# Lower weight halves of q, k, v and the gates by an adding DMA, in place of a GpSimd subtraction

## The chip, the cores and the metric

The kernel runs on one core of a Trainium2 chip. The metric is the device time of one execution in microseconds (us). TensorE (PE) multiplies, VectorE (DVE) and ScalarE (ACT) work element by element, GpSimd (POOL) does so as well, and SyncE (SP) only issues DMAs here. Every engine works through its own instructions in order; what it needs from another engine or from a DMA it waits for on a semaphore, and everything behind the waiting instruction waits with it.

## What is computed

One layer of a hybrid encoder on 512 tokens of width 1024, float32. A projection `w_in` (1024 x 4096) of the modulated, normalised input gives q, k, v, the input u of a state-space branch and two sets of gates. The part that the change touches is this:

```python
h = _normalize(x) * (1.0 + sc_m) + sh_m
proj = h @ w_in
q, k, v, u, g_sb, g_ssm = jnp.split(proj, IN_SPLITS, axis=-1)
y_sb = stick_breaking_attention(q, k, v) @ w_sb_up
y_ssm = s5_branch(u, ...) @ w_ssm_up
merged = jax.nn.sigmoid(g_sb) * y_sb + jax.nn.sigmoid(g_ssm) * y_ssm
y = merged @ w_out
```

After it come a residual with layer norm, a SwiGLU channel mixer of hidden width 2816, and a second residual with layer norm.

## The kernel before

**Splitting.** TensorE multiplies in a rounded float32 form (F32R). To keep accuracy each operand is taken as a sum of an upper part (the value rounded to F32R) and a lower part (the value less the upper part), and `mm3` (L151 on) makes three matmuls of each product: upper by upper, upper by lower, lower by upper; all stand on L149 in the trace.

**Units of weights.** `unit` (L170) brings in 512 KB of weights as a tile of 128 x 1024 float32, `raw`, by a DMA of SP (L146), has ACT round it into `whi` (L177, a cast) and an engine given by the caller write `wlo = raw - whi` (L159, `sub`). There are 8 `raw` buffers (shared with the modulation weights `ra` and with tiles `ce` of the state-space branch) and 4 each of `whi` and `wlo`. A `raw` buffer is free for the next load when the last reader is done with it. All loads stand on SP in the program's order.

**Stages.** Until about 94 us: layer norm, modulation, the columns of u, and the first q and k tiles, beside the sines and cosines of the state-space branch, whose arguments DVE prepares (L395 to L472) and ACT evaluates (L424, L425). From 94 to about 180 us: four state-space slices (`ssm_slice`, L561: complex products on DVE and POOL at L555 to L558, two scans on DVE at L642 and L643), and between them q, k and v. From there to about 340 us: four pairs of attention heads; after each head two gate tiles (`gate_tile`); from 266 us pieces of later modulation vectors on DVE (`ada_acc`, L244). Then merge, GLU, up and out projections, and from 470 us the channel mixer.

**Who gets what.** `qk_tile` (6 units), `v_tiles` (2 x 2 units) and `gate_tile` (16 units) hand `G`, which is GpSimd, to `unit`: 26 units in all. I number the gate tiles 0 to 15. GLU, up, out and the channel mixer hand in engines by tables (`ENG`, `FENG`), mostly DVE. A scheduler places each instruction by priorities (streams "ssm", "qkv", "feed", "attn", "gates" and others) and by its own cost estimates, so the order on an engine can move when an instruction is replaced.

Of the kernel before, what the change touches and what calls it, by code (L numbers as in the profile page):

```python
# [16 lines left out]
AF = mybir.ActivationFunctionType  # L17
ALU = mybir.AluOpType

P = 128  # L20
# [61 lines left out]
def _build(tc, I, out):  # L82
    nc = tc.nc
    V, G = nc.vector, nc.gpsimd
    tt, ts, stt = V.tensor_tensor, V.tensor_scalar, V.scalar_tensor_tensor
    act, acopy = nc.scalar.activation, nc.scalar.copy
    cnt = [0]

    def nm(s):
        cnt[0] += 1  # L90
        return f"{s}_{cnt[0]}"
# [4 lines left out]
    @contextmanager  # L96
    def prio(name):

        old = tc.cur_priority
        tc.cur_priority = streams[name]  # L100
        yield
        streams[name] = tc.cur_priority
        tc.cur_priority = old
# [28 lines left out]
    def get(dt=F32):  # L132

        i = places.popleft()
        ap = const.tile([P, 512], dt, tag=f"s{i}", name=nm(f"s{i}"))
        tiles[id(ap)] = (i, ap)
        return ap

    def put(*aps):
        for ap in aps:  # L140
            places.append(tiles.pop(id(ap))[0])
# [3 lines left out]
    def load(o, i):  # L145
        return tc.keep_in_program_order(nc.sync.dma_start(out=o, in_=i))  # L146
# [4 lines left out]
    def mm3(o, a, b, start, stop):  # L151

        r = mm(o, a[0], b[0], start, False)
        mm(o, a[0], b[1], False, False)
        mm(o, a[1], b[0], False, stop)
        return r

    def sub(dst, a, b, eng=V):
        return eng.tensor_tensor(dst, a, b, ALU.subtract)  # L159

    def split(x, n=512, eng=V, keep=False):

        h, l = get(F32R), get(F32R)
        acopy(h[:, :n], x[:, :n])  # L164
        sub(l[:, :n], x[:, :n], h[:, :n], eng)
        if not keep:
            put(x)
        return h, l

    def unit(view, a, b, eng=V):  # L170

        with prio("feed"):
            raw = wp.tile([P, D], F32, tag="raw", name=nm("raw"), bufs=NRAW)
            load(raw.rearrange("p (a b) -> p a b", a=a), view)
            hi = wp.tile([P, D], F32R, tag="whi", name=nm("whi"), bufs=NHI)
            lo = wp.tile([P, D], F32R, tag="wlo", name=nm("wlo"), bufs=NHI)
            acopy(hi, raw)  # L177
            sub(lo, raw, hi, eng)
        return hi.rearrange("p (a b) -> p a b", a=a), lo.rearrange("p (a b) -> p a b", a=a)

    def slot_unit(view, a, b, eng=V):
# [11 lines left out]
    w_in, w_glu, w_up, w_sb = rows128(I["w_in"]), rows128(I["w_glu"]), rows128(I["w_ssm_up"]), rows128(I["w_sb_up"])  # L193
# [103 lines left out]
    with prio("first"):  # L297
# [11 lines left out]
        hT = hpairs  # L309
# [205 lines left out]
    def fbank():  # L515
        fcnt[0] += 1
        return banks[6 + fcnt[0] % 2]

    def fm_one(view, h, K=KC, o=None, eng=V):

        w = unit(view, K, P, eng) if K == KC else view
        o = fbank() if o is None else o
        for kc in range(K):
            mm3(o, [x[:, kc, :] for x in w], h[kc], kc == 0, kc == K - 1)
        return o
# [6 lines left out]
    def evac_q(p_, i, dst, scale):  # L532
        with prio("feed"):
            act(dst[i], p_, AF.Copy, scale=scale)
# [131 lines left out]


    def qk_tile(i):
        o = fm_one(w_in[:, :, 256 + P * i:256 + P + P * i], hT, eng=G)
        if i < 2:  # L670
            evac_q(o, 2 + i, qT, 0.125)
        else:
            evac_q(o, i - 2, kT, 1.0)

    def v_tiles(i):
        us = [unit(w_in[:, k:k + 4, 1024 + 256 * i:1280 + 256 * i], 4, 256, G) for k in (0, 4)]
        for m2 in range(2):
            o = fbank()
            for m in range(2):
                tk = slice((2 * m2 + m) * P, (2 * m2 + m + 1) * P)  # L680
                for kc in range(KC):
                    mm3(o[:, m * 256:(m + 1) * 256], [a[:, tk] for a in hT[kc]],
                        [x[:, kc % 4, :] for x in us[kc // 4]], kc == 0 and m == 0, kc == KC - 1)
            with prio("feed"):
                for h in range(2):
                    acopy(vT[2 * i + h].rearrange("p (k c) -> p k c", k=NT)[:, 2 * m2:2 * m2 + 2, :],
                          o.rearrange("p (m c) -> p m c", m=2)[:, :, h * P:(h + 1) * P])

    def gate_w(i):
        col = (3072, 2048)[i // 8] + P * (i % 8)  # L690
        return w_in[:, :, col:col + P]
# [4 lines left out]
    def gate_tile(i, eng):  # L696
        lst = (gs, gb)[i // 8]
        o = fm_one(gate_w(i), hT, eng=eng)
        with prio("feed"):
            g = gpre.pop(0) if gpre else get()  # L700
            acopy(g, o)
        lst.append(g)

    with prio("ssm"):
        ys = []
    dense = [lambda i=i: qk_tile(i) for i in range(6)] + [lambda i=i: v_tiles(i) for i in range(2)]
    for s in range(4):
        with prio("ssm"):
# [69 lines left out]
    def later(at):  # L778

        with prio("later"):  # L780
            for _ in range(LATER.get(at, 0)):
                i = len(pieces)
                pieces.append(at)
                if i % 2 == 0:
                    (gm_acc if i < 4 else sf_acc).append(get())
                if i < 4:
                    ada_gate(2, i, gm_acc[i // 2][:, i % 2 * 256:i % 2 * 256 + 256])
                    continue
                j = i - 4
                ada_acc(sf_acc[j // 2][:, j % 2 * 256:j % 2 * 256 + 256], w_ada[:, :, 3 * D + j * 256:3 * D + j * 256 + 256], 256)  # L790
# [3 lines left out]
    for hp in range(4):  # L794
        with prio("attn"):
            at = get()

            q_, k_, kl = ([get(F32R), get(F32R)] for _ in range(3))
            for a in range(2):
                r, r2 = HEAD[a], HEAD[1 - a]  # L800
                acopy(q_[a][r, :], qT[hp][r, :])
                sub(q_[a][r2, :], qT[hp][r, :], q_[a][r, :])
                acopy(k_[a][r, :], kT[hp][r, :])
                acopy(k_[a][r2, :], kT[hp][r, :])
                sub(kl[a][r, :], kT[hp][r, :], k_[a][r, :])
                sub(kl[a][r2, :], kT[hp][r, :], k_[a][r, :])
            put(qT[hp], kT[hp])
            vs = [get(F32R), get(F32R)]
            for a in range(2):
                v4 = vs[a].rearrange("p (k a d) -> p k a d", k=NT, a=2)  # L810
                src = vT[hp].rearrange("p (k c) -> p k c", k=NT)[:, :, 64 * a:64 * a + 64]
                acopy(v4[:, :, 0, :], src)
                sub(v4[:, :, 1, :], src, v4[:, :, 0, :])
            put(vT[hp])
        for a in range(2):
            with prio("attn"):
                for i, (q0, layout) in enumerate(HALVES):
                    half_head(a, q_, k_, kl, vs, at, q0, layout, banks[3 * a + i:3 * a + 1 + 2 * i])
            for g in range(2):
                i = 4 * hp + 2 * a + g  # L820
                with prio("gates"):
                    gate_tile(i, G)
                later(("gate", i))
        put(*q_, *k_, *kl, *vs)
        with prio("attn"):
            attnT.append(split(at))
# [24 lines left out]
    with prio("mix"):  # L851
# [4 lines left out]
        for m in range(4):  # L856
            if m % 2 == 0:
                w = unit(glu_w[m // 2], 4, 256)
            o = bk.get()
            fm_one([x[:, :, m % 2 * P:(m % 2 + 1) * P] for x in w], yS, 4, o)  # L860
            g = get()
            sigmoid(g, o, bias=bglu[:, m:m + 1])
            bk.put(o)
            tt(g, g, yT[m], ALU.mult)
            yG.append(split(g))
            later(("glu", m))
# [4 lines left out]
        for i in range(4):  # L871
            w = unit(up_w[i][0], 4, 256)
            for m in range(2):
                g = gs[2 * i + m]
                sigmoid(g, g)
                o = bk.get()
# [4 lines left out]
            for m in range(2):  # L881
                g, g2 = gb[2 * i + m], gs[2 * i + m]
                sigmoid(g, g)
                o = bk.get()
# [403 lines left out]
```

## Time and profile before

| quantity | value |
|---|---|
| time, median of 3 runs | 841.86 us (839.55 to 842.65) |
| the profiled execution: its time | 841.87 us |
| its span in the trace | 840.2 us |
| PE busy | 760.7 us (91%) |
| DVE busy | 637.8 us (76%) |
| ACT busy | 416.7 us (50%) |
| POOL busy | 190.9 us (23%) |
| mean granted TensorE clock | 0.966 |

The profiled execution lies 0.01 us from the median, so lengths of its trace can be set against the median as they are; 1.7 us of its time lie outside the span. The page also gives the span in 40 slices, the chain of work that ended last, the costliest groups of instructions and the DMAs. Further views of the trace give the busy time by stage, one engine's instructions in order of time with what ended its idle time, and one tile's instructions.

### The profile page before, as it was taken

To read this page: it belongs to the slowest core of one execution; us is meant where nothing else is said; L and a number is where in the kernel's file an instruction comes from. 1 tells how busy PE (TensorE), PEld (TensorE's weight loads), DVE (VectorE), ACT (ScalarE), POOL (GpSimd) and SP (SyncE) were. 2 spreads that over 40 slices of the span, in tenths; PEclk is the share of its full clock that TensorE was granted. 3 is DMA by queue.
4 is the path that set the end of the run, shared out by engine and by line. 5 is a ranking of instruction groups with operands and counts; after the bars stand their busy time and mean duration, and the time that the engine had idled before them with its cause. 6 is when DMAs were issued, how large, how long until landed. Compare 5 with 4: busy or idle time off the path is not lost.

```text
span 840.2 us, 12264 instructions
## 1 busy us (share of the span) xinstructions
PE 760.7 (91%) x4767; PEld 667.5 (79%) x4767; DVE 637.8 (76%) x975; ACT 416.7 (50%) x689; POOL 190.9 (23%) x161
## 2 busy tenths in 40 slices
PE   3969896899999888699998589999999999999995
PEld 2858686897888577588886589999999999888884
DVE  5599778789677998688879988767778777533267
ACT  4234623454887665883526294444445556632211
POOL 1451626662532443100464000000000000000013
PEclk9989999899999999899999699999999999999998
DMA  9960004420002471770972003414445334441001
GB/s 275 354 176 26 1 1 136 116 76 26 1 1 83 147 228 53 240 251 28 348 238 87 0 2 102 150 52 151 151 152 181 116 107 150 148 154 48 1 26 75
DMA packets 95754, 97.86 MB, mean 116 GB/s; under 512 B 4040, under 2 KB 85968, under 8 KB 95696
## 3 DMA queue, kind: packets, MB, share of 16 engines
q1 hardware_dynamic: 95552, 96.82, 36.6%
q8 instruction: 37, 0.61, 0.3%
q10 hardware_dynamic: 144, 0.26, 0.1%
q14 instruction: 21, 0.17, 0.1%
HBM read 94.97 MB, written 2.10 MB: 116 GB/s over the span
## 4 chain that ended last, share of the span: by engine, by line
PE 61%; DVE 24%; issue 4%; ACT 4%; DMA 4%; SPq 2%; POOL 1%; POOLq 0%; DVEq 0%; ACTq 0%
PE b L149 60%; DVE s L244 3%; DVE s L159 2%; SPq L146 2%; DVE s L469 1%; DMA s<-w_in 1%; DMA ra<-w_ada 1%; DVE s L621 1%; DVE wlo L159 1%; DVE raw L1042 1%; ACT s L424 1%; DVE s L642 1%; DVE s L402 1%; DVE st L280 1%; ACT s L425 1%
## 5 line engine op out<-in xcount | busy, mean ns | idle before, releaser
L149 PE MATMUL b<-h,whi 128*128 128x256 f32 (+1 forms) x896 | 217.4, 332 | 18.8 <-DVE h L159 9.4
L159 DVE TENSOR_TENSOR wlo<-raw,whi 128x1024 fp32r<-128x1024 f32 x103 | 129.5, 1264 | 69.1 <-ACT whi L177 37.1
L149 PEld LDWEIGHTS b<-h,whi 128*128 128x128 f32 x896 | 151.2, 191 | 33.4 <-DVE h L159 9.6
L149 PE MATMUL b<-s,whi 128*128 128x256 f32 (+1 forms) x800 | 166.7, 307 | 6.7 <-ACT whi L177 6.7
L149 PE MATMUL b<-h,wlo 128*128 128x256 f32 (+1 forms) x448 | 147.9, 331 | 0.0
L149 PEld LDWEIGHTS b<-s,whi 128*128 128x128 f32 x800 | 129.5, 190 | 16.6 <-ACT whi L177 7.0
L149 PE MATMUL b<-whi,s 128*128 128x512 f32 (+1 forms) x392 | 122.5, 390 | 0.0
L149 PE MATMUL b<-s,wlo 128*128 128x256 f32 (+1 forms) x400 | 121.2, 305 | 0.8 <-DVE wlo L159 0.8
L159 DVE TENSOR_TENSOR s<-s,s 128x512 fp32r<-128x512 f32 (+4 forms) x112 | 89.2, 802 | 37.0 <-PE b L149 18.1
L1049 ACT CAST whi<-raw 128x1024 fp32r<-128x1024 f32 x70 | 72.7, 1050 | 75.5 <-PE b L149 43.3
L177 ACT CAST whi<-raw 128x1024 fp32r<-128x1024 f32 x66 | 68.9, 1048 | 80.9 <-PE b L149 66.2
L159 POOL TENSOR_TENSOR wlo<-raw,whi 128x1024 fp32r<-128x1024 f32 x33 | 84.5, 2572 | 63.5 <-ACT whi L177 62.7
L149 PEld LDWEIGHTS b<-h,wlo 128*128 128x128 f32 x448 | 85.6, 191 | 7.2 <-POOL wlo L159 0.4
L1228 POOL TENSOR_TENSOR s<-s,s 128x512 f32<-128x512 f32 x6 | 8.6, 1431 | 356.6 <-DVE s L1227 356.6
L149 PE MATMUL b<-s,s 128*128 128x128 f32 (+2 forms) x438 | 81.9, 317 | 6.1 <-DVE s L159 3.8
L149 PEld LDWEIGHTS b<-whi,s 128*128 128x128 f32 x392 | 73.3, 188 | 16.6
L164 ACT CAST s<-s 128x512 fp32r<-128x512 f32 (+1 forms) x106 | 57.8, 570 | 49.4 <-DVE s L744 13.7
L149 PEld LDWEIGHTS b<-s,s 128*128 128x128 f32 x438 | 68.8, 192 | 15.9 <-DVE s L159 4.4
L149 PEld LDWEIGHTS b<-s,wlo 128*128 128x128 f32 x400 | 75.3, 188 | 4.5 <-DVE wlo L159 1.0
L149 PE MATMUL b<-wlo,s 128*128 128x512 f32 (+1 forms) x196 | 76.5, 390 | 0.0
L244 DVE SCALAR_TENSOR_TENSOR s<-ra,ca,s 128x256 f32<-128x256 f32 x88 | 58.3, 681 | 2.8 <-DMA ra<-w_ada 2.2
L159 POOL TENSOR_TENSOR s<-s,s 128x512 fp32r<-128x512 f32 (+1 forms) x32 | 39.5, 1246 | 78.9 <-ACT s L164 56.1
(244 smaller groups left out, 1111.8 us busy)
## 6 DMA issues: line engine op xcount, KB each, us to landing
raw<-w_ffn_in SPq DMA_DIRECT2D x44, 512.0 KB, 4.3
ra<-w_ada SPq DMA_DIRECT2D x32, 512.0 KB, 6.0
raw<-w_in SPq DMA_DIRECT2D x26, 512.0 KB, 4.7
raw<-w_ffn_out SPq DMA_DIRECT2D x22, 512.0 KB, 3.4
wa<-w_ada SPq DMA_DIRECT2D x12, 512.0 KB, 7.7
raw<-w_out SPq DMA_DIRECT2D x12, 512.0 KB, 6.3
s<-x SPq DMA_DIRECT2D x16, 256.0 KB, 4.2
wa<-w_ada SPq DMA_DIRECT2D x8, 256.0 KB, 4.9
```

What stands on the lines that cost most here:

```text
L146: return tc.keep_in_program_order(nc.sync.dma_start(out=o, in_=i))
L149: return nc.tensor.matmul(o, lhsT, rhs, start=start, stop=stop, skip_group_check=True, **kw)
L159: return eng.tensor_tensor(dst, a, b, ALU.subtract)
L164: acopy(h[:, :n], x[:, :n])
L177: acopy(hi, raw)
L244: stt(dst, r_, ca[:, k:k + 1], init if k == 0 else dst, ALU.mult, ALU.add)
L280: V.bn_stats(st[:, i, :], x)
L402: e.scalar_tensor_tensor(p_, n, -c, p_, ALU.mult, ALU.add)
L424: act(o, a, AF.Abs, bias=b)
L425: sins.append(act(o, o, AF.Sin, scale=-1.0, bias=hpi_c))
L1049: acopy(hi, x)
L1228: G.tensor_tensor(z[h], z[h], l2b[h], ALU.add)
```

## The change

For the 26 units of q, k, v and the gates the callers hand in `None`. `unit` then lets ACT write the negated rounded value into `wlo` (an ACTIVATE with scale -1), and GpSimd issues a DMA that reads `raw` and adds it onto `wlo`. The sum is `raw - whi`, as before. GpSimd's 26 subtractions go; 26 ACT instructions and 26 DMAs on GpSimd's queue come. Five lines of code come in, one of them blank, so every line below shows a number higher by 5 after the change.

```diff
             acopy(hi, raw)
-            sub(lo, raw, hi, eng)
+            if eng is None:
+                act(lo, raw, AF.Copy, scale=-1.0)
+                G.dma_start(out=lo, in_=raw, accum_op=ALU.add)
+            else:
+                sub(lo, raw, hi, eng)
...
-        o = fm_one(w_in[:, :, 256 + P * i:256 + P + P * i], hT, eng=G)
+        o = fm_one(w_in[:, :, 256 + P * i:256 + P + P * i], hT, eng=None)
...
-        us = [unit(w_in[:, k:k + 4, 1024 + 256 * i:1280 + 256 * i], 4, 256, G) for k in (0, 4)]
+        us = [unit(w_in[:, k:k + 4, 1024 + 256 * i:1280 + 256 * i], 4, 256, None) for k in (0, 4)]
...
-                    gate_tile(i, G)
+                    gate_tile(i, None)
```

The order on SP stays as it is. On the others three places matter.

GpSimd, where the third pair of q and k tiles and the second slice's `ce` tiles (its output matrices) are prepared. Before, the two subtractions stand ahead of four memsets:

```order
L159 TENSOR_TENSOR wlo_1365<-raw_1362,whi_1364 128x1024 [waits PE_49,DMAHW5_49,Activation_49,Pool_49]
L159 TENSOR_TENSOR wlo_1396<-raw_1393,whi_1395 128x1024 [waits DMAHW6_49,PE_49,Activation_49]
L614 MEMSET s_155_943 128x512 [waits DVE_49]
L595 MEMSET ce_1458 128x640 [waits Pool_49]
L595 MEMSET ce_1460 128x640 [waits Pool_49]
L569 MEMSET s_170_1062 128x512 [waits PE_49,Activation_49]
```

Now, with the DMAs in their place:

```order
L619 MEMSET s_155_943 128x512 [waits DVE_49,PE_49,Pool_49]
L181 DMA wlo_1369<-raw_1366 128x1024 [waits DMAHW5_49,PE_49,Activation_49]
L600 MEMSET ce_1464 128x640 [waits DMASW4_49,DMASW2_49]
L181 DMA wlo_1401<-raw_1398 128x1024 [waits DMAHW6_49,PE_49,Activation_49]
L600 MEMSET ce_1466 128x640 [waits DMASW5_49,DMASW3_49]
L574 MEMSET s_170_1064 128x512 [waits PE_49]
```

The memset of s_155 moved ahead; each `ce` memset, whose buffer was a `raw` one, now waits for adding DMAs to land (DMASW), one of which was issued by the row just ahead of it.

TensorE, at the first v unit (whi_1545, wlo_1546; after the change whi_1551, wlo_1552). Before:

```order
L149 MATMUL b_70<-ce_1098,s_186_1113 128x128
L149 MATMUL b_73<-whi_1545,h_64 128x256 [waits Activation_49]
L149 MATMUL b_72<-whi_1545,h_64 128x256 [waits Activation_49]
L149 MATMUL b_73<-wlo_1546,h_64 128x256 [waits Pool_49]
L149 MATMUL b_73<-whi_1545,h_65 128x256
```

Now:

```order
L149 MATMUL b_70<-ce_1100,s_186_1115 128x128
L149 MATMUL b_73<-whi_1551,h_64 128x256 [waits Activation_49]
L149 MATMUL b_72<-whi_1551,h_64 128x256
L590 MATMUL b_70<-ident,s_136_861 128x128 [waits Activation_49]
L590 MATMUL b_70<-ident,s_136_861 128x128 x3
L149 MATMUL b_73<-wlo_1552,h_64 128x256 [waits DMASW6_49]
```

The first matmul on the lower part waits for the adding DMA, and four small transposes have moved ahead of it.

ACT, at the end of the sines and cosines and the evacuation of the first q tile (L534 brings finished q tiles out of PSUM: s_114 and s_115, whose columns were multiplied with u's, then s_116, the first `qk_tile`). Before, the row of L534 that empties b_71 is followed by the small copies of L543 and then by the next cast:

```order
L534 ACTIVATE s_115_840<-b_71 128x512 [waits PE_49]
L543 COPY s_135_860<-b_69 128x4x32 [waits DVE_49]
L543 COPY s_137_862<-b_66 128x4x32 [waits DVE_49]
L543 COPY s_137_862<-b_67 128x4x32 [waits DVE_49]
L543 COPY s_137_862<-b_68 128x4x32 [waits DVE_49]
L543 COPY s_137_862<-b_69 128x4x32 [waits DVE_49]
L177 CAST whi_1364<-raw_1362 128x1024 [waits DMAHW5_49,PE_49,Pool_49]
```

Now:

```order
L539 ACTIVATE s_115_840<-b_71 128x512 [waits PE_49]
L548 COPY s_137_862<-b_66 128x4x32 [waits DVE_49]
L548 COPY s_137_862<-b_67 128x4x32 [waits DVE_49]
L610 COPY s_153_931<-s_138_881 128x512 [waits DVE_49,Pool_49]
L178 CAST whi_1368<-raw_1366 128x1024 [waits DMAHW5_49,PE_49]
L539 ACTIVATE s_116_841<-b_73 128x512 [waits PE_49]
```

A copy that belongs to the first slice, s_153, now stands ahead of the cast and of the evacuation that frees b_73.

## Rows read from the trace of the kernel before

**Rows 1.** Busy us by stage (PE, PEld, DVE, ACT, POOL), granted clock, DMA share, GB/s:

```profile
42.00:96.00 54.00, 42.81 (x226) 34.94 (x224) 49.48 (x132) 27.34 (x48) 20.87 (x19) 0.91 0.28 79
96.00:134.00 38.00, 36.41 (x206) 31.34 (x206) 28.49 (x47) 15.23 (x28) 18.50 (x19) 0.96 0.09 28
134.00:206.00 72.00, 62.25 (x424) 57.59 (x424) 62.64 (x82) 30.61 (x56) 39.62 (x30) 0.93 0.32 89
206.00:268.00 62.00, 61.52 (x348) 53.80 (x349) 43.02 (x64) 50.33 (x98) 25.17 (x18) 1.00 0.01 2
268.00:340.00 72.00, 61.91 (x302) 50.40 (x301) 65.57 (x103) 46.68 (x89) 28.42 (x19) 0.95 0.51 153
```

**Rows 2.** GpSimd's subtractions until 345 us: durations in ns (min/median/max), starts, and who waited:

```profile
L159 POOL TENSOR_TENSOR wlo<-raw,whi x26: 2342/2409/3207, 49.2 to 317.4; 128x1024 fp32r<-128x1024 f32 x26
...
who waited for it (us, times):
...
  PEld b L149: 2.1, 2
  PE b L149: 1.5, 1
```

**Rows 3.** DVE in order of time, 49 to 58 us: start, us, instruction, count:

```profile
49.28 7.82 DVE L469 TENSOR_SCALAR s<-s,s 128x128 f32<-128x128 f32 x5
...
57.96 0.27 DVE L469 TENSOR_SCALAR s<-s,s 128x128 f32<-128x128 f32 x1
```

**Rows 4.** DVE groups by form, 48 to 345 us: busy us, mean ns, idle before:

```profile
L244 DVE SCALAR_TENSOR_TENSOR s<-ra,ca,s 128x256 f32<-128x256 f32 x53 | 40.1, 775 | 2.6 <-DMA ra<-w_ada 2.2
...
L469 DVE TENSOR_SCALAR s<-s,s 128x128 f32<-128x128 f32 x16 | 13.1, 902 | 0.0
```

**Rows 5.** The chain that ended last, 42 to 100 us: start, us, what:

```profile
74.52 1.34 ACT s L424 x2
...
87.49 0.31 DVE s L483
...
95.71 0.51 ACT s L534
96.26 4.10 PE b L149 x11
```

**Rows 6.** DVE in order of time from 95.5 us, at the first slice's products:

```profile
95.89 5.13 DVE L555 TENSOR_TENSOR s<-s,s 128x256 f32<-128x256 f32 x2
```

**Rows 7.** PE in order of time, 134 to 148 us, with idle time and its releaser:

```profile
134.16 0.39 PE L149 MATMUL b<-wlo,h 128*128 128x256 f32 x1 [1.50 <-POOL wlo L159]
...
147.59 1.11 PE L578 MATMUL b<-ident,s 128*128 128x128 f32 x4 [4.37 <-DVE s L558]
```

**Rows 8.** Busy us in the stretch with the longest of these waits, columns as in rows 1:

```profile
145.00:152.00 7.00, 4.41 (x21) 4.41 (x22) 6.85 (x13) 1.72 (x4) 1.60 (x2) 0.51 0.27 75
```

**Rows 9.** PE in order of time, 276 to 302 us:

```profile
276.50 0.74 PE L149 MATMUL b<-h,whi 128*128 128x512 f32 x2 [1.83 <-ACT whi L177]
...
278.95 0.79 PE L149 MATMUL b<-h,wlo 128*128 128x512 f32 x1
...
301.45 0.56 PE L149 MATMUL b<-s,s 128*128 128x256 f32 x3 [3.40 <-DVE s L159]
```

**Rows 10.** DVE in order of time, 279 to 285 us:

```profile
279.57 4.95 DVE L244 SCALAR_TENSOR_TENSOR s<-ra,ca,s 128x256 f32<-128x256 f32 x3
...
284.92 0.47 DVE L244 SCALAR_TENSOR_TENSOR s<-ra,ca,s 128x256 f32<-128x256 f32 x1
```

**Rows 11.** The page's group of `whi` casts: busy us, mean ns, idle before:

```profile
L177 ACT CAST whi<-raw 128x1024 fp32r<-128x1024 f32 x66 | 68.9, 1048 | 80.9 <-PE b L149 66.2
```

**Rows 12.** DMA issues by tile: count, KB each, median us from issue to landing:

```profile
raw<-w_in SPq DMA_DIRECT2D x26, 512.0 KB, 4.7
raw<-w_ffn_out SPq DMA_DIRECT2D x22, 512.0 KB, 3.4
...
raw<-w_ssm_up SPq DMA_DIRECT2D x4, 512.0 KB, 8.2
```

## The prediction

> **What bounds the kernel now.** I read the busy time by stage first [rows 1]. TensorE fills 61.52 of 62 us between 206 and 268 us and 36.41 of 38 between 96 and 134: there nothing else matters. It idles 11.2 us from 42 to 96, 9.75 from 134 to 206 and 10.1 from 268 to 340, and in each of these the granted clock is below 1 too. What it idles for is seen in its instructions in order of time: mostly DVE, 4.37 us in one place, 3.40 in another [rows 7, 9]. Why DVE is late is seen in DVE's own rows: an L469 that takes 0.27 us takes 1.56 on average in a row of five [rows 3], an L244 takes 1.65 beside 0.47 [rows 10]. Each such stretch lies on top of a subtraction of GpSimd, of which there are 26 of 2.41 us from 49 to 317 us [rows 2]. GpSimd is hardly disturbed (its longest is 3.21), DVE all but stops. So the change removes 26 x 2.41 = 62.7 us in which DVE could not use two inputs, and brings a transfer that GpSimd issues, whose length no row shows.
>
> **The new chain of a unit.** Cast, negated copy, DMA. The copy has the cast's size, so 1.05 us [rows 11]. For the landing D of an adding DMA of 512 KB I take bounds from the plain loads of that size [rows 12]: at the low end 3.4 us, the shortest median; at the high end 16.4, twice the 8.2 of the slowest, since the adding DMA must bring in two pieces of 512 KB. I take 6.8, twice 3.4: that load has rows of 4 KB, as `raw` to `wlo` has, while the slower ones have short rows. GpSimd's subtraction took 2.4, so a unit whose lower part is used at once is late by 1.05 + D - 2.4 = D - 1.35: 5.45 us, from 2.05 to 15.05.
>
> The Trainium skill bears on D: in "DMA: Bandwidth & Descriptors", section "Anatomy of one DMA", a GpSimd-issued DMA is fitted by 2.0 us plus the bytes over 436 GB/s. For 512 KB this would be an estimate of 3.2 us, and the sum below would then end near 827. The fit is of transfers that don't add, and no row here shows one that does.
>
> **Where the later arrival shows.** For most units nowhere: of 26 lower parts TensorE's matmuls waited for one and its weight loads for two [rows 2]; counted unit by unit, those of q and k lie ready 16 us or more before use, and those of the gates until 268 us 14 or more. Two places have no slack. At the first v unit TensorE waits 1.50 us for the subtraction [rows 7]; its load waits for a buffer, so nothing brings it forward. At gate tile 10, the first after 268 us, TensorE waits 1.83 us for the cast, and the lower part is used at 278.95 [rows 9], within 0.1 us of its being ready. Gate tiles 11 to 15 have 3 to 7 us, which 5.45 about uses up. So two units pay: 2 x (D - 1.35) = 10.9 us.
>
> **What comes back, stage by stage.**
>
> 42 to 96 us. DVE's 16 L469 take 13.1 us [rows 4] where 16 x 0.27 = 4.3 would do: 8.8 gone. So the first sine can start on ACT at about 65.7 instead of 74.52 [rows 5]. What is late next: the last piece of h, which ACT gets from TensorE, and 4 negated copies (4.2 us) on ACT. I let the sines end at 79 instead of 87.49, and the first slice's products follow, ready near 89.7 since two L555 no longer take 5.13 us [rows 6]. But ACT now has the copy s_153, which waits for these products, ahead of the cast and of the evacuation that frees b_73: 89.7 + 0.5 + 1.0 + 0.5 = 91.7 (copy and evacuation as L534's 0.51, the cast) against 96.26, when TensorE begins the next tile [rows 5, 11]. Gain 4.6, between 2 (the copy late) and 8 (the whole stall).
>
> 96 to 134. TensorE is full; the gain is carried. The first v unit: -5.45, balance -0.8. GpSimd's two `ce` memsets wait for landings that it has itself just asked for, 2D = 13.6 us instead of 4.9 of subtractions; the second slice needs them some 30 us later, so this costs nothing unless D nears 15.
>
> 134 to 206. Idle 9.75 us and 0.07 of 72, 5.0, of lost clock [rows 1]: after the 4.37 us wait the granted clock is 0.51, the lower of its two levels (1.2 of 2.4 GHz), for 7 us [rows 7, 8]. The idle is DVE's chain of slices, which loses its stops. A wait of 5 us at the v unit will bring the low clock once more: 7 us at half speed cost 3.4. So 9.75 + 5.0 - 3.4 = 11.4 at most; I take 10. Balance +9.2.
>
> 206 to 268. DVE's stops are hidden here, TensorE being full. ACT has 50.33 of 62 and gets four negated copies, 4.2 us, between exponentials that TensorE's order rests on: -1. Balance +8.2. Gate tile 10: -5.45, balance +2.8.
>
> 268 to 340. DVE is busy 65.57 of 72 us. The 53 L244 take 40.1 us where 0.47 each makes 24.9 [rows 4, 10]: 15.2 of stops, of which part stays, as GpSimd keeps the subtractions of the attention weights. I count 11.7 at the units. TensorE's idle for DVE, such as 3.40 us [rows 9], and the lost clock (0.05 x 72 = 3.6) are about 11; I let half come back, 5. Balance +7.8. Loads of the later pieces, which come through 8 shared buffers, are the next to be late.
>
> After 340 only 7 subtractions of GpSimd are left, untouched, and all is shifted as it is. Sum: 4.6 + 10 - 1 + 5 - 10.9 = +7.7, and 841.9 - 7.7 is about 834 us. The ends of D give 14.5 faster (827) and 11.5 slower (853). These lengths are of an execution of 841.87 us, 0.01 from the median, so the sum is taken from the median as it is.
>
> **The rivals.**
>
> All of DVE's stops come back. If D is near 3.4 (14.5) and the two stages with 9.75 + 5.0 and 10.1 + 3.6 us of idle and clock return most of it, 3 to 10 us more: 815 to 825, say 820. For it: the chain of waits runs through DVE almost without a break in both. Against it: buffers and loads are close behind.
>
> The landing is late. From 18.6 = 2 (D - 1.35), that is D = 10.7, the two waits eat what the four stages give. At D = 13 they cost 23.3, gate tiles 11 to 15, with their 3 to 7 us, each wait some more, and the low clock follows each wait: 847 to 855, say 850, slower. For it: SP's loads run beside, a load with 8.2 us is in the rows, and the units are read twice. Against it: the share of time in which the 16 DMA engines are busy is only 0.27 to 0.32 there [rows 1, 8].
>
> GpSimd's issuing is held up by DVE. In this kernel: if the issue must find a gap in DVE's work, which is busy 62.64 of 72 and 65.57 of 72 us with instructions of 0.27 to 1.65 us back to back [rows 1, 3, 10], each DMA is late by several of them, 2 to 5 us: D = 9 to 12, 838 to 845 by the sum, say 842. Its only row here speaks against it: GpSimd's subtractions, run into by DVE all the time, took 3.21 at most beside 2.41 [rows 2]. The Trainium skill, "SBUF — State Buffer", section "Who interferes with whom", has this as a rule: a DMA "stalled" by a DVE op was one issued by GpSimd, whose writing of descriptors is starved. No row of before shows such a DMA.
>
> The change doesn't do what it says. If issuing occupies GpSimd as the subtraction did, DVE's stops remain by half: 18.6 / 2 - 10.9 = 1.6 slower, 843.5.
>
> **How the numbers follow.** A change of 0.5%, 4.2 us, is about what a measurement of this kernel can tell from none. The forecast, 828 to 838, has 0.40. All stops return, 0.16, also faster. No difference by a half-done removal or by DVE holding up the issue, 0.12 and 0.08. Slower, by a late landing 0.19 and by DVE holding it up further 0.05. So faster 0.56, same 0.20, slower 0.24. The range reaches from 818, in the middle of the first rival, to 850, the middle of the late landing; about 0.08 and 0.10 are outside.
>
> **What would show it.** In the changed kernel's profile L469, L555, L637 and L244 must fall to their short durations; an L244 of 1.6 us on a landing refutes the main step. ACT's group of negated copies must be 26 of about 1.05 us. At the first v unit and at gate tile 10 TensorE's wait for the DMA must be about 5 us longer than the wait before; each gives D, cast's end to wait's end less 1.05. TensorE should start the second q tile at about 92 us, and the stage that ran from 134 to 206 be shorter by about 10. The prediction is wrong if D is over 10, if the DMAs of GpSimd queue behind each other, or if DVE's stops were only where TensorE did not wait.

## The result, and the profile after

The changed kernel takes 831.05 us (median of 4 runs, 828.48 to 832.43) where the kernel before takes 841.17 us beside it; the ratio is 0.9877, with a 95% interval of 0.9843 to 0.991. Run once more beside later experiments it gave 0.9895 (0.9877 to 0.9913). It is about 1.1% faster. The forecast was 834, the range 818 to 850. The profiled execution is the shortest of its four, 828.48 us with a span of 826.8, so its trace shows some 2.5 us more gain than the median does.

The busy times by stage (columns as in rows 1) stand against [rows 1]:

```profile
42.00:96.00 54.00, 46.50 (x244) 38.20 (x245) 44.17 (x143) 34.95 (x59) 18.01 (x20) 0.94 0.53 123
96.00:134.00 38.00, 33.48 (x197) 28.80 (x196) 25.83 (x48) 15.04 (x27) 13.56 (x18) 0.95 0.30 69
134.00:206.00 72.00, 72.00 (x499) 67.00 (x499) 45.78 (x85) 50.48 (x85) 25.49 (x31) 0.98 0.70 156
206.00:268.00 62.00, 57.75 (x304) 48.75 (x303) 39.48 (x71) 50.75 (x99) 16.70 (x18) 0.94 0.33 83
268.00:340.00 72.00, 60.66 (x286) 48.97 (x287) 44.32 (x87) 49.92 (x86) 17.23 (x18) 0.89 0.72 197
```

From 134 to 206 us TensorE no longer idles at all (72.00 of 72, before 62.25), and DVE is busy 45.78 us where it was 62.64, though it makes more instructions. From 268 to 340 DVE falls from 65.57 to 44.32, but TensorE's busy time does not rise and its granted clock falls to 0.89.

DVE's groups by form from 48 to 345 us answer [rows 4]; the lines are 5 higher:

```profile
L249 DVE SCALAR_TENSOR_TENSOR s<-ra,ca,s 128x256 f32<-128x256 f32 x54 | 26.8, 520 | 2.6 <-DMA ra<-w_ada 1.9
...
L474 DVE TENSOR_SCALAR s<-s,s 128x128 f32<-128x128 f32 x16 | 3.7, 287 | 0.0
L560 DVE TENSOR_TENSOR s<-s,s 128x256 f32<-128x256 f32 x8 | 3.7, 474 | 10.7 <-ACT s L610 8.7 <-PE b L149 2.0
L642 DVE TENSOR_TENSOR s<-s,s 128x512 f32<-128x512 f32 x4 | 2.8, 688 | 0.0
```

The last two lines are the other two that the prediction named, L555 and L637; before, in the same view:

```profile
L555 DVE TENSOR_TENSOR s<-s,s 128x256 f32<-128x256 f32 x8 | 8.4, 1066 | 5.0 <-ACT s L605 4.9
L637 DVE TENSOR_TENSOR s<-s,s 128x512 f32<-128x512 f32 x4 | 4.9, 1232 | 0.0
```

The 16 small products take 3.7 us in place of 13.1, the modulation pieces 26.8 for 54 in place of 40.1 for 53. The stops by the 26 units are gone. The prediction had named an L244 of 1.6 us on a landing as what would refute it, and there is one piece of this length, at 271.65 us, while an adding DMA is under way (270.01 to 274.54). But it lies on two of GpSimd's subtractions of the attention weights, which the change leaves as they were (DVE, then GpSimd):

```profile
271.65 1.79 DVE L249 SCALAR_TENSOR_TENSOR s<-ra,ca,s 128x256 f32<-128x256 f32 x1
```

```profile
270.58 2.58 POOL L159 TENSOR_TENSOR s<-s,s 128x512 fp32r<-128x512 f32 x2
```

The pieces at 269.70 and 270.23 us, on the same landing, take 0.49 us each, so it doesn't refute. What came in their place is seen by the tile `wlo`, until 345 us (the counts, durations in ns, who waited for whom, and the time from issue to landing):

```profile
L180 ACT ACTIVATE wlo<-raw x26: 1050/1057/1087, 48.9 to 309.5; 128x1024 fp32r<-128x1024 f32 x26
L181 POOL DMA_DIRECT2D wlo<-raw x26: 833/866/2042, 50.2 to 310.9; - x26
...
  POOL ce L600: 9.3, 3
  PEld b L149: 5.1, 3
  PE b L149: 4.0, 3
...
DMA to landing us min/median/max: 4.5/5.0/8.1
```

The copy costs the 1.05 us that was assumed. The landing, which no row of before showed, is 5.0 us in the median, between the low end of 3.4 and the 6.8 that I took. TensorE waits for a lower part three times. The first is at the first v unit (start, us, instruction, idle before it); it answers [rows 7]:

```profile
127.07 0.48 PE L149 MATMUL b<-whi,h 128*128 128x256 f32 x2
131.33 1.12 PE L590 MATMUL b<-ident,s 128*128 128x128 f32 x4 [3.78 <-ACT s L623]
132.73 0.58 PE L149 MATMUL b<-wlo,h 128*128 128x256 f32 x1 [0.28 <-DMA wlo<-raw]
```

The long part of the wait is not put down to the DMA but to ACT's copies at L623, which the transposes ahead of the lower part need. ACT's rows say why they are late:

```profile
125.79 1.04 ACT L178 CAST whi<-raw 128x1024 fp32r<-128x1024 f32 x1 [1.25 <-DMA raw<-w_in]
126.74 1.05 ACT L180 ACTIVATE wlo<-raw 128x1024 fp32r<-128x1024 f32 x1
127.70 1.03 ACT L178 CAST whi<-raw 128x1024 fp32r<-128x1024 f32 x1
128.64 1.05 ACT L180 ACTIVATE wlo<-raw 128x1024 fp32r<-128x1024 f32 x1
129.60 1.41 ACT L623 COPY s<-b 32x512 f32<-32x512 f32 x3
```

Two negated copies stand ahead of them, 2.1 us. Had they been early, TensorE would have waited for the landing instead, which came 1.4 us after them. The stretch that follows runs mostly at the lower level of the clock (1.2 of 2.4 GHz), 0.54 in the mean, which over 7.5 us loses 3.5 (columns as in rows 1; first the changed kernel, then e9, an experiment below in which that wait is gone):

```profile
130.00:137.50 7.50, 5.88 (x27) 5.48 (x28) 7.36 (x15) 1.24 (x4) 0.84 (x1) 0.54 0.94 203
```

```profile
130.00:137.50 7.50, 7.50 (x67) 7.50 (x66) 7.34 (x17) 3.08 (x6) 0.00 (x0) 1.00 0.50 143
```

The other two waits for a lower part are at gate tiles 10 and 12; the first answers the row at 278.95 of [rows 9]:

```profile
269.49 0.80 PE L149 MATMUL b<-h,wlo 128*128 128x512 f32 x1 [0.29 <-DMA wlo<-raw]
...
297.77 0.80 PE L149 MATMUL b<-h,wlo 128*128 128x512 f32 x1 [3.40 <-DMA wlo<-raw]
```

To see where time was won, I set the starts of the same matmuls side by side (us; e5, e9, e10 and e8 are experiments below). A scheduler may move other work past such a mark, so single steps of one or two microseconds say little; in the trace of e11, the changed kernel run again, the lower part of gate tile 10 is used at 271.45 us, 2.0 later than here.

| mark on TensorE | before | after | e5 | e9 | e10 | e8 |
|---|---|---|---|---|---|---|
| third q/k tile, first matmul | 96.26 | 91.59 | 91.54 | 91.91 | 91.57 | 91.91 |
| first v unit, first with the lower part | 134.16 | 132.73 | 128.46 | 129.07 | 129.00 | 128.16 |
| gate tile 0, first matmul | 181.00 | 169.39 | 160.98 | 160.25 | 160.21 | 160.86 |
| gate tile 3, first matmul | 209.67 | 194.79 | 185.97 | 185.98 | 185.94 | 185.96 |
| gate tile 9, first matmul | 261.07 | 246.17 | 237.75 | 237.02 | 236.98 | 234.68 |
| gate tile 10, first with the lower part | 278.95 | 269.49 | 261.10 | 267.38 | 264.47 | 267.96 |
| gate tile 15, end | 338.55 | 329.22 | 311.13 | 326.13 | 313.59 | 312.71 |
| first GLU matmul | 349.26 | 335.56 | 322.56 | 335.05 | 331.91 | 334.46 |

### The profile page after: what moved, and what is told of

Its sections match the earlier page's. It is cut to its first block, busy times and chain, and to the rows that moved or that the text cites. A ratio compares the mean times of both kernels' runs of the same rounds, so it can differ in the third digit from the quotient of the medians.

```text
span 826.8 us, 12325 instructions
## 1 busy us (share of the span) xinstructions
PE 761.7 (92%) x4767; PEld 667.0 (81%) x4767; DVE 585.1 (71%) x975; ACT 438.5 (53%) x715; POOL 147.2 (18%) x161
## 3 DMA queue, kind: packets, MB, share of 16 engines
q1 hardware_dynamic: 95552, 96.82, 37.2%
## 4 chain that ended last, share of the span: by engine, by line
PE 51%; DVE 4%; ACT 2%; issue 2%; DMA 1%; POOL 0%; SPq 0%; POOLq 0%; DVEq 0%; ACTq 0%
PE b L149 51%; DVE st L285 1%; DMA raw<-w_glu 1%; ACT s L974 0%; DVE s L972 0%; ACT whi L1054 0%; DVE mv L290 0%; DVE h L159 0%; DVE s L946 0%; ACT s L844 0%; DVE s L1232 0%; POOL s L159 0%; DVE s L955 0%; DVE s L943 0%; ACT s L1074 0%
## 5 line engine op out<-in xcount | busy, mean ns | idle before, releaser
L149 PE MATMUL b<-h,whi 128*128 128x256 f32 (+1 forms) x896 | 217.9, 333 | 13.1 <-DVE h L159 8.2
L159 DVE TENSOR_TENSOR wlo<-raw,whi 128x1024 fp32r<-128x1024 f32 x103 | 127.5, 1243 | 72.2 <-ACT whi L178 38.9
L149 PEld LDWEIGHTS b<-s,whi 128*128 128x128 f32 x800 | 128.6, 189 | 16.5 <-ACT whi L178 5.7
L159 DVE TENSOR_TENSOR s<-s,s 128x512 fp32r<-128x512 f32 (+4 forms) x112 | 79.0, 716 | 59.4 <-PE b L149 22.1
L149 PEld LDWEIGHTS b<-whi,s 128*128 128x128 f32 x392 | 73.2, 188 | 16.5
L1047 DVE TENSOR_TENSOR raw<-raw,raw 128x1024 f32<-128x1024 f32 x40 | 48.6, 1220 | 5.8 <-DMA raw<-w_ffn_in 5.6
L249 DVE SCALAR_TENSOR_TENSOR s<-ra,ca,s 128x256 f32<-128x256 f32 x88 | 45.3, 533 | 2.8 <-DMA ra<-w_ada 1.9
```

Source lines behind the costliest of these rows:

```text
L149: return nc.tensor.matmul(o, lhsT, rhs, start=start, stop=stop, skip_group_check=True, **kw)
L249: stt(dst, r_, ca[:, k:k + 1], init if k == 0 else dst, ALU.mult, ALU.add)
L1047: tt(r, x, y, ALU.add)
```

## The experiments

The theory that the prediction went by, called A in the expectations: the gain is DVE freed from GpSimd's subtractions, the cost is a lower part that arrives late where it is wanted at once. All ratios are to the kernel before, run on the same chip.

| run | what it is | us | ratio, 95% interval |
|---|---|---|---|
| e1 | DMAs for the gates alone | 835.88 | 0.9950 (0.9934 to 0.9966) |
| e2 | DMAs for q, k, v alone | 836.45 | 0.9945 (0.9920 to 0.9969) |
| e3 | changed, with an unused GpSimd subtraction | 861.80 | 1.0264 (1.0239 to 1.0288) |
| e4 | changed, with unused GpSimd fills | 833.85 | 0.9925 (0.9902 to 0.9948) |
| e5 | changed, without the adding DMAs | 816.37 | 0.9711 (0.9689 to 0.9734) |
| e6 | gate tiles 10 to 15 on DVE | 831.34 | 0.9874 (0.9847 to 0.9901) |
| e7 | gate tiles 10 to 15 on GpSimd | 833.65 | 0.9920 (0.9895 to 0.9946) |
| e8 | all 26 on DVE | 827.35 | 0.9837 (0.9819 to 0.9855) |
| e9 | v on DVE | 828.06 | 0.9850 (0.9827 to 0.9873) |
| e10 | v and gate tiles 10 to 15 on DVE | 827.23 | 0.9839 (0.9823 to 0.9855) |
| e11 | the changed kernel again | 832.32 | 0.9895 (0.9877 to 0.9913) |
| e12 | e10 with GLU's weights loaded earlier | 824.84 | 0.9816 (0.9789 to 0.9843) |

### The two halves of the change (e1, e2)

e1:

```diff
-        o = fm_one(w_in[:, :, 256 + P * i:256 + P + P * i], hT, eng=None)
+        o = fm_one(w_in[:, :, 256 + P * i:256 + P + P * i], hT, eng=G)
...
-        us = [unit(w_in[:, k:k + 4, 1024 + 256 * i:1280 + 256 * i], 4, 256, None) for k in (0, 4)]
+        us = [unit(w_in[:, k:k + 4, 1024 + 256 * i:1280 + 256 * i], 4, 256, G) for k in (0, 4)]
```

> Adding DMAs for the 16 gate units alone; q, k and v keep GpSimd's subtraction. Theory A (the gain is DVE freed from GpSimd's subtractions; the cost is a late lower part at gate tile 10 and after): comparing the two traces by the start of the same matmuls, the gates' part gains 3.3 us between 181 and 268 us, loses 5.4 at gate tile 10, wins nothing until 340 and 4 us after; so 1 to 4 us faster than the kernel before, 837 to 840. DVE's L469 of 128x128 keep their mean near 0.9 us. Rival B (what helps is only that GpSimd's queue is shorter for the attention weights it splits, so the gates carry the gain): 6 to 10 us faster, 831 to 835.

e2:

```diff
-                    gate_tile(i, None)
+                    gate_tile(i, G)
```

> Adding DMAs for the 10 units of q, k and v alone; the gates keep GpSimd's subtraction. Theory A: the first gate tile starts 11.6 us earlier than in the kernel before, as in the changed kernel; the gates' 3.3 us until 268 are missing, the 5.4 at gate tile 10 are not paid, so 10 to 13 us faster than before, 828 to 831, the same as the changed kernel. Rival B: 1 to 4 us faster only.

Each half gives about half of the gain, 4.6 and 4.0 us; together 8.6, near the 10.1 and the 8.1 of the whole. Both expectations of A missed, e1 by a little and e2 by over 5 us; e2's 4.0 us is what rival B had named. I had read the halves off the marks of the two traces and given all that was won by gate tile 0 to q, k and v. But the subtractions of the first gate tiles are made while the state-space slices still run. GpSimd's rows of e2 show them there:

```profile
154.59 2.40 POOL L159 TENSOR_TENSOR wlo<-raw,whi 128x1024 fp32r<-128x1024 f32 x1 [2.77 <-ACT whi L178]
158.45 2.56 POOL L159 TENSOR_TENSOR wlo<-raw,whi 128x1024 fp32r<-128x1024 f32 x1 [1.46 <-ACT whi L178]
```

DVE's rows of e2 show two products of a slice stopped there, beside their like that take 0.4 us:

```profile
154.63 2.64 DVE L561 TENSOR_TENSOR s<-s,s 128x256 f32<-128x256 f32 x1
...
158.81 2.49 DVE L563 TENSOR_TENSOR s<-s,s 64x256 f32<-64x256 f32 x1
```

They stop DVE's work on the slices, not on the gates' own stage, and in e2 gate tile 0 starts at 174.88 us, between the 181.00 of before and the 169.39 of after. DVE's durations go with the halves, as A says: in e1 the 16 small products take 12.1 us and the modulation pieces 28.3, in e2 3.6 and 37.7. But the times of the halves don't tell A from B; the next two runs do.

### GpSimd as busy as before, reading or only writing (e3, e4)

e3:

```diff
             if eng is None:
+                sub(lo, raw, hi, G)
                 act(lo, raw, AF.Copy, scale=-1.0)
```

> As the changed kernel, but GpSimd also makes its old subtraction into the same lower tile first, and ACT then overwrites it: the result of the subtraction is not used. Theory A: DVE's stops are all back (L469 near 0.9 us mean, L244, now L249, near 0.78) and the late landing is paid as well, 2.4 us later: 842 to 852. Rival C (the stops did not matter; the gain is from the order that the scheduler found): 831 to 837.

e4:

```diff
             if eng is None:
+                for _ in range(2):
+                    G.memset(lo.bitcast(F32), 0.0)
                 act(lo, raw, AF.Copy, scale=-1.0)
```

> As the run before this one, but in place of the unused subtraction GpSimd fills the lower tile twice with zeros, about 2.1 us of GpSimd per unit that write the memory and do not read it; ACT overwrites it. Theory A: DVE is hardly stopped (L469 near 0.29, L249 near 0.52), so most of the gain stays: 829 to 836. Rival B (GpSimd's queue): as slow as with the unused subtraction, 840 to 852.

861.80 and 833.85 us. What GpSimd was given, by the tile `wlo`, first e3, then e4:

```profile
L159 POOL TENSOR_TENSOR wlo<-raw,whi x26: 2352/2406/3293, 48.7 to 331.6; 128x1024 fp32r<-128x1024 f32 x26
```

```profile
L181 POOL MEMSET wlo<- x52: 942/954/1605, 38.4 to 294.8; 128x1024 f32 x52
```

That is 2.41 and 1.91 us of GpSimd per unit. DVE's groups by form, again e3 (its pieces run on behind 345 us, where the rows stop) and then e4:

```profile
L250 DVE SCALAR_TENSOR_TENSOR s<-ra,ca,s 128x256 f32<-128x256 f32 x46 | 38.2, 851 | 1.8 <-DMA ra<-w_ada 1.1
L475 DVE TENSOR_SCALAR s<-s,s 128x128 f32<-128x128 f32 x16 | 12.5, 856 | 0.0
```

```profile
L251 DVE SCALAR_TENSOR_TENSOR s<-ra,ca,s 128x256 f32<-128x256 f32 x54 | 30.0, 577 | 5.1 <-DMA ra<-w_ada 4.6
L476 DVE TENSOR_SCALAR s<-s,s 128x128 f32<-128x128 f32 x16 | 7.5, 805 | 0.0
```

With the subtraction the modulation pieces are at 0.85 us and the 16 products at 12.5 us in all, near the kernel before; with the fills at 0.58 and 7.5. The mean of 0.58 is not the fills' doing: only three of e4's pieces lie on a fill, and they take 0.48 us each; all that take over 0.49 us lie on subtractions of the attention weights. The clearest rows for a fill are those of the first slice's products, which took 5.13 us beside subtractions [rows 6]; here two of the same form run while GpSimd fills (DVE, then GpSimd, in e4):

```profile
95.57 0.76 DVE L563 TENSOR_TENSOR s<-s,s 128x256 f32<-128x256 f32 x2
```

```profile
95.51 1.84 POOL L181 MEMSET wlo<- 128x1024 f32 x2
```

So rival B, GpSimd's queue, falls: e4 gives GpSimd four fifths of e3's work, though ahead of the cast and so at other times, and keeps two thirds of the gain. Rival C, the order, falls with e3, which has the changed kernel's instructions and DMAs and is slower than before; e3's own order is not quite the changed kernel's, but e8 below, with neither GpSimd's subtractions nor DMAs and in another order again, keeps the gain. A's range for e3, 842 to 852, was missed by 10 us. Not all of e3's 21 us are stops. Its subtraction stands behind the cast, so the landing comes 2.4 us later still, where the fills of e4 are made ahead of the cast; at the first v unit the lower part is used at 145.74 us in e3, 136.20 in e4. The clean reading is at the third q/k tile, whose lower part lies ready long before: 97.75 us in e3, 94.04 in e4, 91.59 in the changed kernel.

The Trainium skill has this rule in "SBUF — State Buffer", section "Who interferes with whom": a DVE instruction with two SBUF inputs contends with a GpSimd instruction that reads SBUF, not with one that only writes it. The rows of instructions with two full inputs agree with it: 5.13 us for two products beside subtractions, 0.76 beside fills. The 16 small products, which have one full input, are another matter (last section).

### What the landing still costs (e5, e9, e11)

e5 leaves the addition out, so the lower part is only the negated rounded value and the result is not the layer's:

```diff
                 act(lo, raw, AF.Copy, scale=-1.0)
-                G.dma_start(out=lo, in_=raw, accum_op=ALU.add)
```

> The changed kernel without its 26 adding DMAs: the lower part stays the negated rounded value, so the result is not the layer's; the rest of the work is the same. Theory A (what the change still pays is the landing, where a lower part is used at once): the waits at the first v unit and at gate tiles 10 to 13 go, 3 to 4 us at the first and about 5 at the others, so 5 to 10 us faster than the changed kernel, 821 to 826. Rival D (the landing is covered, and the changed kernel is bound by DVE and ACT between 96 and 340): no difference, 829 to 833.

816.37 us, beyond both expectations: 14.7 us below the changed kernel. By the marks 8.4 us of it are there by gate tile 0, which puts the price of the first v unit near that. e9 takes the landing away at v alone, by DVE's own subtraction:

```diff
-        us = [unit(w_in[:, k:k + 4, 1024 + 256 * i:1280 + 256 * i], 4, 256, None) for k in (0, 4)]
+        us = [unit(w_in[:, k:k + 4, 1024 + 256 * i:1280 + 256 * i], 4, 256, V) for k in (0, 4)]
```

> The changed kernel with the 4 units of v on DVE; q, k and the 16 gates keep the adding DMA. Theory A: the first v unit no longer waits for ACT's negated copies and a landing, which cost 8 to 9 us between there and the first gate tile (160.98 us without the DMAs, 169.39 with them, by the start of its first matmul): the first gate tile starts at 159 to 162. Of this the attention stage, where TensorE idles for ACT and DVE, gives back a part: 824 to 828 in all, 3 to 7 us faster than the changed kernel. Rival F (it was the order that changed, not the wait): first gate tile at 167 to 171, 829 to 833.

e11 is the changed kernel beside e9 and e10:

> The changed kernel itself, on the chip of the two runs before it: 828 to 833 by both theories. It gives the others their difference from it.

828.06 against 832.32 us, and the intervals of the ratios do not meet (0.9827 to 0.9873, 0.9877 to 0.9913). Rival F's times did not come. TensorE at the first v unit and at gate tile 0 in e9:

```profile
129.07 0.39 PE L149 MATMUL b<-wlo,h 128*128 128x256 f32 x1 [0.66 <-DVE wlo L159]
...
160.25 0.63 PE L149 MATMUL b<-h,whi 128*128 128x512 f32 x2
```

The wait is 0.66 us instead of 3.78 and 0.28, and gate tile 0 starts 9.1 us earlier than in the changed kernel's trace. But in e9, and in e5, the four transposes no longer stand ahead of the first lower part, and in e9 ACT is spared v's copies too, so neither run parts the wait for the landing from these. What speaks for the landing is the changed kernel's own trace: it came at 132.7 us, and in either order the lower part could not be used before it.

Of the 9.1, 4.3 remain in the medians, as A expected. The traces don't show where: at the first GLU matmul e9 is 0.5 us ahead, and both spans are 826.8 us (the changed kernel's trace is its shortest execution). Most of the lead is given back between gate tiles 9 and 10: at gate tile 9 e9 is still 9.2 us ahead, at the first upper matmul of gate tile 10 (261.58 us, after 264.21) 2.6. There e9's TensorE waits 3.56 us for that tile's cast, whose load has only just come: SP issued it at 252.59 us, in the changed kernel at 254.83, in both behind the loads of the first later piece, whose tile GpSimd must clear first.

### The gate tiles after 268 us (e6, e7, e8, e10, e12)

e6 and e7 take `V` and `G` there:

```diff
-                    gate_tile(i, None)
+                    gate_tile(i, V if i > 9 else None)
```

> The changed kernel with gate tiles 10 to 15 on DVE (a subtraction of about 1.24 us, no adding DMA). Theory A: their lower parts are ready 1.05 + 5.0 - 1.24, about 4.8 us, earlier, which takes the waits at gate tiles 10 and 12 away; DVE, busy 44 of 72 us there, has room for the 7.4 us: 3 to 6 us faster than the changed kernel, 825 to 828. Rival E (DVE's chain sets the end of that stage, and takes the 7.4 us back): 831 to 835.

```diff
-                    gate_tile(i, None)
+                    gate_tile(i, G if i > 9 else None)
```

> The changed kernel with gate tiles 10 to 15 on GpSimd as before. Theory A: no wait for a landing at gate tile 10, but six subtractions stop DVE's L249 again, about 2 us each; the two are near each other, 829 to 834. Rival D (the landing is covered): the stops come on top, 835 to 840.

831.34 and 833.65 us: neither is told from the changed kernel by its time. E's number came, its reason did not quite. In e6 the waits for the landing go, and gate tile 15 ends at 321.32 us, 7.9 before the changed kernel's 329.22; but the first GLU matmul starts at 338.34, 2.8 after it. The gain at the gate tiles is lost behind them. In e7 gate tile 10's lower part is used at 268.50 us, where the changed kernel's is at 269.49, so by this trace that landing cost about a microsecond there; against e11's 271.45, where TensorE waits 1.65 us for it, 3.0.

e8 gives all 26 units to DVE (the three calls hand in `V`):

> All 26 lower parts by DVE, neither GpSimd's subtractions nor adding DMAs. DVE is not stopped, but gets 26 x 1.24 = 32 us of work where it had some 50 us of stops, and a lower part is ready 1.24 us after its cast. Theory A: a part of the gain, most of it where GpSimd's stops lay on the chain: 832 to 839. Rival C (only the order matters): could be anywhere; near or over 841 would say that DVE's time is worth as much as its stops.

827.35 us, faster than A expected; its interval overlaps that of the changed kernel's first measurement, not that of e11. DVE's own subtractions (31 with those of GLU and up), by form until 345 us:

```profile
L159 DVE TENSOR_TENSOR wlo<-raw,whi 128x1024 fp32r<-128x1024 f32 x31 | 39.1, 1260 | 9.8 <-ACT whi L178 9.5
```

At 1.26 us each they cost less than GpSimd's 2.41 cost DVE in stops, and ACT is spared 26 copies. So the change gains by what it removes; the adding DMA is one of two ways to do without GpSimd here, and by e11 the slower, by some 5 us. e10 keeps it only where a lower part has 14 us or more to spare:

```diff
-        us = [unit(w_in[:, k:k + 4, 1024 + 256 * i:1280 + 256 * i], 4, 256, None) for k in (0, 4)]
+        us = [unit(w_in[:, k:k + 4, 1024 + 256 * i:1280 + 256 * i], 4, 256, V) for k in (0, 4)]
...
-                    gate_tile(i, None)
+                    gate_tile(i, V if i > 9 else None)
```

> v and gate tiles 10 to 15 on DVE, the adding DMA only for q, k and gate tiles 0 to 9, whose lower parts are wanted 14 us or more after they are ready. Theory A: no exposed landing is left and DVE is spared 20 us of the 32 that it has with all 26 units: as the run before this one at the first gate tile, gate tile 15 done at 313 to 318, and 821 to 827 in all, the same as or faster than all on DVE. Rival G (after gate tile 10 the end is set by the weights of GLU, whose loads wait behind the last attention work of GpSimd): the gain at gate tile 15 is lost in a wait for these weights of 4 us or more, 826 to 831.

827.23 us: as e8, and where A's range ends and G's lies. Gate tile 15 ends at 313.59 us, as A expected, 15.6 before the changed kernel's; the first GLU matmul starts at 331.91, only 3.7 before. Rival G names the reason, GLU's weights:

```profile
331.91 1.65 PE L149 MATMUL b<-s,whi 128*128 128x512 f32 x3 [4.35 <-ACT whi L178]
```

Their loads stand on SP behind those of ln1, which wait for tiles of the last attention work. e12 moves the loads of ln1 behind the up projections:

```diff
-        l1g, l1b = bcast("ln1_g"), bcast("ln1_b")
...
         for x in yG + attnT:
             put(*x)
+        l1g, l1b = bcast("ln1_g"), bcast("ln1_b")
```

> As the kernel with v and gate tiles 10 to 15 on DVE, and the four loads of ln1's scale and offset moved behind those of the up projections, so that the weights of GLU no longer wait behind them. Rival G (the gain at the last gate tiles is lost in the wait for GLU's weights, 4.35 us there): 4 to 8 us faster than without the move, 819 to 823. Against G (the attention work that is left behind the last gate tile sets that end): 826 to 829, with TensorE waiting for DVE or ACT instead.

824.84 us, the fastest that gives the layer's result, 2.4 below e10 by medians, though the intervals overlap; it lies between the range of G, 819 to 823, and that against G, 826 to 829. The same matmul in e12's trace:

```profile
327.28 0.96 PE L149 MATMUL b<-s,whi 128*128 128x512 f32 x3 [0.96 <-ACT s L164]
```

The wait for the weights is gone, and TensorE waits 0.96 us for ACT's split of the other input instead. G has part of it: the mark moves by 4.6 us, but ahead of it TensorE still idles 3.12 us for ACT's GELU at L839, which the code keeps behind the last exponentials of the attention. So the attention work left behind gate tile 15 sets that end as well.

## Why the prediction was right, by its own steps

**The main step held.** DVE's stops were GpSimd's subtractions; the profile after shows the short durations that were named. For instructions with two full inputs e4's rows show that reading is what counts, not how long GpSimd works. Two readings of it were loose. "Could not use two inputs" doesn't describe L469, which has one full input and a scalar per partition, and which fills slow as well. And the row of three L244 in 4.95 us [rows 10] lies on a subtraction of the attention weights too (279.24 to 281.68 us), which the change leaves; the unit's, from 281.84, stopped one of the three, 2.64 us.

**42 to 96 came out link by link.** The first sine starts at 65.10 us (65.7 was forecast), the sines end at 78.3 (79), and ACT's rows show the copy of s_153, the cast and the evacuation as they were added up, with TensorE's next tile at 91.59 (91.7):

```profile
89.47 0.62 ACT L610 COPY s<-s 128x512 f32<-128x512 f32 x1 [0.35 <-DVE s L563]
90.00 1.04 ACT L178 CAST whi<-raw 128x1024 fp32r<-128x1024 f32 x1
90.94 0.59 ACT L539 ACTIVATE s<-b 128x512 f32<-128x512 f32 x1
```

The prediction calls that tile the second q tile; it is the third of `qk_tile`.

**The terms, in the order of the sum:**

| term | forecast, us | measured |
|---|---|---|
| 42 to 96: third q/k tile | +4.6 | +4.7 (96.26 to 91.59) |
| first v unit | -5.45 | -3.2 (+4.7 to +1.4) |
| 134 to 206: to gate tile 3 | +10 | +13.5 (+1.4 to +14.9) |
| 206 to 268: to gate tile 9 | -1 | 0 (+14.9 to +14.9) |
| gate tile 10's lower part | -5.45 | -5.4 (+14.9 to +9.5) |
| 268 to 340: to gate tile 15's end | +5 | -0.1 (+9.5 to +9.3) |
| to the first GLU matmul | 0 | +4.4 (+9.3 to +13.7) |
| sum | +7.7 | 13.4 by the spans, 10.1 by the medians |

That 831.05 came out so near 834 is in part luck: by the marks 268 to 340 gave 5.1 us less than its term, and the v unit, 134 to 206 and the way to GLU together 10.1 more.

**D was too long.** I took 6.8 us as two plain transfers; it is 5.0. By the forecast's own formula a unit is then late by D - 1.35 = 3.65, and the mark at the first v unit lost 3.2. Two of the named signs failed here: TensorE's wait at the first v unit was to be about 5 us longer than before and is 2.6 (4.06 against 1.50), and at gate tile 10 it is 0.29. The wait itself was not as described: ACT's two negated copies held up transposes that the scheduler had put ahead of the lower part, and the landing came just behind. I had counted the copies as ACT time that lies free, and not asked what stands behind them on ACT at that place. Its whole price up to gate tile 0 was near what was charged in two terms, 5.45 and 3.4 for the low clock: 8.4 to 9.1 us by e5 and e9, which also move the transposes.

**134 to 206 was sized too low.** My upper end was 11.4. The idle time did go in full (72.00 busy of 72), and the mark won 13.5. The marks near it scatter: the gain in all is 14.9 at gate tile 3, 16.5 at 4, 15.1 at 5.

**Gate tile 10 was right by accident.** The mark lost 5.4, but 2.6 of it ahead of its first upper matmul, and the profile puts only 0.29 us to the landing. e7, which has no landing there, uses the lower part 1 to 3 us earlier. What holds this mark is its load: in e9 and e10, 9 us ahead at gate tile 9, the advance shrinks to 2 to 5 us here too. What I read as a wait for a cast before [rows 9] was a wait for that load already, as ACT's row of the kernel before shows, and I did not follow it back to what the load waits for:

```profile
275.41 1.04 ACT L177 CAST whi<-raw 128x1024 fp32r<-128x1024 f32 x1 [1.97 <-DMA raw<-w_in]
```

**268 to 340: the cost was elsewhere than at tile 10.** At tile 12 the landing took 8.1 us, and TensorE waited 3.40 us. It ran beside loads of the later pieces on SP; that these made it long was not tried. I had noted that tiles 11 to 15 have 3 to 7 us to spare and that D would use them up, but charged nothing; with the stops gone from DVE its loads come closer together, as I read the DMA share of 0.72 (before 0.51, without adding DMAs). What was won came behind it: at the first GLU matmul TensorE waits 3.80 us, before 6.70.

**The rivals.** The late landing did not come (the longest is 8.1 us, 8.7 in e11; the turning point was 10.7). That DVE would hold up GpSimd's issuing by 2 to 5 us did not come either: 0.87 us to issue one in the median, 2.04 at most (at 54.0 us, among the small products), and a shortest landing of 4.5 us in e3 too, where DVE and GpSimd run into each other. GpSimd's `ce` memsets did wait for landings, 9.3 us in three waits, and as forecast this cost TensorE nothing: it has no idle time over half a microsecond between 93 and 127 us. A gain of 17 to 27 us (815 to 825), all stops turned into time, was not reached. e5, without additions, comes to 25 us, but no kernel here that gives the layer's result does: the best, e12, gains 15.

**What stays open.** e5 is 11 us faster than e10 and 8.5 faster than e12, though these have no exposed landing. By the marks e10 is 3.4 us behind e5 at gate tile 10's lower part, 2.5 at the end of gate tile 15 and 9.4 at the first GLU matmul, so most arises between these last two, where more of the attention work is left in e10. e10 also has DVE make the subtractions behind gate tile 10. Whether DVE's 7.6 us for them, the load, or the order decide was not tried. Nor was why GpSimd's fills slow a DVE instruction with one full input.

## What to carry to other kernels

When an engine off the critical path seems free, look at what the critical one's instructions cost while it runs: here 2.4 us of GpSimd's subtraction cost DVE about 2 us wherever one of the stopped instructions lay on it, and giving GpSimd's work to DVE itself, at 1.26 us, was faster. A long transfer in place of a short instruction is free only where the product lies ready longer than the landing; sort the uses by that slack, and take the engine for those that have none. Before charging a wait to its releaser, follow the load behind it: two of the gains here, e9's and e10's, ended at a load that waits in line behind others.

## What the runs showed that was not expected

An adding DMA from one place of the memory onto another costs the transfer engines more than a load. The DMA queues of the changed kernel (kind, packets, MB, share of 16 engines over the span):

```profile
q1 hardware_dynamic: 95552, 96.82, 37.2%
q0 software_dynamic: 3744, 13.63, 8.9%
```

For the 26 adding DMAs 8.9% of 826.8 us is 2.8 us of all 16 engines per transfer of 0.52 MB; the plain queue needs 37.2% for 96.82 MB, 1.7 us for as much, a mean over all its loads. With a landing of 5.0 us it is neither one transfer (3.4) nor two (6.8). The Trainium skill's fit in "DMA: Bandwidth & Descriptors", section "Anatomy of one DMA", which gives an estimate of 3.2 us, is too short for these adding ones of 5.0.

GpSimd's fills, which only write, did slow one of DVE's instructions: the 16 products at L476 of e4 took 7.5 us, 0.47 each, where they take 0.23 without and 0.82 beside subtractions (13.1 us for 16, [rows 4]). They have one full input. Nine of the 16 lie on a fill by 0.1 us or more, with records of 0.51 to 1.80 us, which overlap one another; the other seven are at 0.27. The three modulation pieces that lie on a fill, with two, take their 0.48.
